# Branch B's tiles: from a turn on TensorE and one store each to a turn in 32x32 blocks on VectorE and four stores each

## The chip, the core and the metric

The kernel runs on one core of a Trainium2 chip. Such a core has engines that run side by side, each through its own list of instructions in order: TensorE (PE in the profile; its weight loads are PEld) multiplies 128x128 blocks into accumulators in PSUM; VectorE (DVE), ScalarE (ACT) and GpSimd (POOL) work on tiles of 128 partitions; SyncE (SP) issues the transfers (DMAs) between the chip's large memory and the tiles. They wait for each other through semaphores. The metric is the device time of one execution in microseconds, the median of several runs.

## What is computed

One layer of an encoder over 2,048 prompt positions and 8 streams of 16 new positions, 2,176 rows of 1,024 channels, or 17 tiles of 128 rows. One projection makes the inputs of three branches; each branch is gated, the three are joined to 1,024 channels, and one output projection with a residual and a normalisation follows. Cut to what matters here:

```python
h = jnp.einsum('btd,de->bte', x, w_in)
a, g_a, u, v, g_b, c1, c2, g_c = jnp.split(h, SPLITS, axis=-1)
y_a = pool_mixer(pool_ext, a, pos0, pool_w, pool_scale)            # 256 channels
v_n = layer_norm(v, gmlp_ln_g, gmlp_ln_b)
y_b = u * spatial_mix(v_n, gmlp_w, gmlp_b)                         # 384 channels
c = c1 * jax.nn.sigmoid(c2)
y_c = conformer_tail(conv_ext, conv_w, conv_b, ...)                # 384 channels, 31 taps
mixed = jnp.concatenate([jax.nn.silu(g_a) * y_a, jax.nn.silu(g_b) * y_b,
                         jax.nn.silu(g_c) * y_c], axis=-1)
out = jnp.einsum('bte,ed->btd', mixed, w_out) + b_out
x_new = layer_norm(ALPHA * x + out, ln_g, ln_b)
```

All inputs are 32-bit floats. Every large product is made of three passes: each operand is split into a high part (a rounded copy, `hi`) and a low part (the rest, `lo`), and hi x hi, lo x hi and hi x lo are summed in one accumulator (`mm3`, lines 208 to 210).

## The kernel before

**Staging.** The 17 tiles are worked in three blocks of 6, 6 and 5 (`BLOCKS`). For each block the program runs through eight groups of projection columns (`GROUPS`): the convolution's inputs (two groups, accumulators `ps_c`), branch A's two (`ps_ga`, `ps_a`), then branch B's v (`ps_v`), its gate (`ps_gb`) and u (`ps_u`), and at last branch C's gate (`ps_gc`). The weights of a group come in pieces through four staging buffers (`stage`), are split by ACT (`whi`, line 152) and VectorE (`wlo`), and are kept in memory (`keep`) for the next blocks. The input columns of the next block come in as `stage<-in_xT` and are split into `xhi` and `xlo` during `ps_gc`.

**Order.** The order of every engine's list is fixed when the program is built. `mm3` advances a clock of TensorE's time; `after(us, fn)` puts a piece of work so many microseconds later on that clock. The convolution's taps (`acc<-cext,cw,acc`, about 1 us each) are kept aside as filling: one is put on VectorE's list whenever a second clock, which sums modelled VectorE times (`Vector`, lines 113 to 130), is behind TensorE's. A `tensor_tensor` of 384 columns counts 0.49 us on it. So any new operation on VectorE moves later taps backwards in the list.

**Branch B.** For tile i of a block, `b_u` multiplies u by the gated mixture (`yb`, rows in the partitions, 384 channels in the columns). For the output projection the channels must be in the partitions. `turn` does this with three 128x128 transposes on TensorE (`tp_b`, line 748); ACT copies the result to `yt` (line 750), and one store puts it into columns 256 to 639 of the tile's row of `mixd` in memory (`store`, line 374). `yb` and `yt` have two buffers each.

**The output stage.** Its start is built into the last block's `ps_gc`: `Mixed` (line 947) loads a tile of `mixd` in two parts of 768 and 256 columns into two staging buffers (line 952) and splits them into `mhi` and `mlo`; then twelve pieces of the output weights come through the same four buffers (`stage<-in_w_out`, line 972; `woxhi`, `woxlo`, `whi`, `wlo`). A load waits until the buffer's last piece is split, so ACT, VectorE and SP go hand in hand here. In ACT's list four of branch C's gates (`sgc`, line 533) stand between these splits. They free accumulators; there are six (`psm`), and the first output product, for two tiles at once, uses four (`ps_o`). SP's list has all loads and stores of the program in one order, among them the last block's convolution states (`o_conv_p`, `o_conv_s`, which wait for ACT's `ncs`).

Of the kernel before, what the change touches and what calls it, by code (L numbers as in the profile page):

```python
# [9 lines left out]
F32 = mybir.dt.float32  # L10
# [4 lines left out]
D = 1024  # L15
P = 128
# [22 lines left out]
BLOCKS = [list(range(0, 6)), list(range(6, 12)), list(range(12, 17))]  # L39
TMAX = 768  # L40
# [33 lines left out]
def encoder_kernel(ctx: ExitStack, tc: tile.TileContext, a):  # L74
    nc = tc.nc
# [5 lines left out]
    pst = ctx.enter_context(tc.tile_pool(name="pst", bufs=2, space=PS))  # L81
# [14 lines left out]
    def after(us, fn):  # L96
        Clock.seq += 1
        heapq.heappush(events, (Clock.pe + us, Clock.seq, fn))
# [35 lines left out]
    vec = Vector()  # L134
# [15 lines left out]
    def split(hi, lo, src, then=None):  # L150

        nc.scalar.copy(hi, src)  # L152

        def low():
            vec.tensor_tensor(out=lo, in0=src, in1=hi.bitcast(F32), op=ALU.subtract)
            if then is not None:
                then()
        if ring.get("ready"):
            after(1.0, low)
        else:  # L160
            low()

    def stage():
        return core.tile([P, TMAX], F32, tag="stage", bufs=STAGE, name="stage")

    class Piece:


        def __init__(self, key, src, cols, keep=None):
            self.key, self.n, self.cols, self.keep = key, src.shape[1], cols, keep  # L170
            self.st = stage()[:, :self.n * cols].rearrange("p (k c) -> p k c", k=self.n)
            nc.sync.dma_start(out=self.st, in_=src)

        def split(self, then=None):
            hi = core.tile([P, 2, 384], F32R, tag="whi", bufs=RING, name="whi")
            lo = core.tile([P, 2, 384], F32R, tag="wlo", bufs=RING, name="wlo")
            split(hi[:, :self.n, :self.cols], lo[:, :self.n, :self.cols], self.st, then)
            ring.setdefault(self.key, []).append((hi, lo))
            if self.keep is not None:
                after(3, lambda: put(self.keep, hi, lo, self.cols))  # L180
# [17 lines left out]
    def wslice(key, k, c0, n):  # L198
        hi, lo = ring[key][k // 2]
        return hi[:, k % 2, c0:c0 + n], lo[:, k % 2, c0:c0 + n]  # L200

    def mm3(outs, kdim=KT, hook=None):

        for k in range(kdim):
            for ps, lhs, rhs in outs:
                lh, ll = lhs(k)
                rh, rl = rhs(k)
                nc.tensor.matmul(ps, lh, rh, start=(k == 0), stop=False)  # L208
                nc.tensor.matmul(ps, lh, rl, start=False, stop=False)  # L209
                nc.tensor.matmul(ps, ll, rh, start=False, stop=(k == kdim - 1))  # L210
            if hook is not None:
                hook(k)
            poll(sum(3 * (o[0].shape[-1] / 2400 + 0.0025) for o in outs))
        Clock.dve = max(Clock.dve, Clock.pe)

    gofs = []
    o = 0
# [28 lines left out]
    class XRow:  # L246
# [14 lines left out]
        def split(self, then=None, halves=False):  # L261
            kp, h = divmod(self.k, 2)
            if h == 0:
                xhi[kp] = core.tile([P, 2, TMAX], F32R, tag=f"xhi{kp}", name=f"xhi{kp}")
                xlo[kp] = core.tile([P, 2, TMAX], F32R, tag=f"xlo{kp}", name=f"xlo{kp}")
            for t in (slice(0, 384), slice(384, self.T)) if halves else (slice(0, self.T),):
                split(xhi[kp][:, h, t], xlo[kp][:, h, t], self.st[:, t], then)

    def xslice(k, t0, n):
        return xhi[k // 2][:, k % 2, t0:t0 + n], xlo[k // 2][:, k % 2, t0:t0 + n]  # L270
# [37 lines left out]
    def C(name, j=0, n=1):  # L308
        return cst[:, CST[name][0] + j:CST[name][0] + j + n]

    ident = const.tile([P, P], F32, name="ident")
# [10 lines left out]
    tmp = tmp_cm.__enter__()  # L322
# [7 lines left out]
    def load_v():  # L330
        nc.sync.dma_start(out=vg, in_=a["gmlp_ln_g"].partition_broadcast(P))
        nc.sync.dma_start(out=vb, in_=a["gmlp_ln_b"].partition_broadcast(P))
        w = raw("wst0", 4)
        nc.sync.dma_start(out=w, in_=a["gw"])
        after(10, lambda: keep_lower(w))
        after(14, lambda: split(*wst, w))
# [32 lines left out]
    mixd = [dram.tile([P, D], F32, name=f"mix{i}") for i in range(NTILE)]  # L369
    stored = {}  # L370

    def store(q, j, src):

        nc.sync.dma_start(out=mixd[q][:, j * P:j * P + src.shape[1]], in_=src)
        stored[q] = stored.get(q, 0) + src.shape[1]

    halo_a = const.tile([P, 2, POOLC], F32, name="halo_a")
    halo_c = const.tile([P, 3, CONVC], F32, name="halo_c")
    nc.gpsimd.memset(halo_a, 0.0)
# [155 lines left out]
    def tail_steps(b):  # L535

        st = {}
# [78 lines left out]
        def pointwise(t0, n, j):  # L616
            nt = n // P
            if j == 0:
                st["m", t0] = cp.tile([P, 3, 3, P], F32, tag="mixs", bufs=1, name="mixs")
            m = st["m", t0]  # L620
            sg = conv_state[(b, "sg")]
            ps = psm.tile([P, 512], F32, tag="mm", name="ps_pw")
            mm3([(ps[:, :n], lambda k: (pwhi[:, k, j * P:(j + 1) * P], pwlo[:, k, j * P:(j + 1) * P]),
                  lambda k: (st["s", t0, k][0][:, :n], st["s", t0, k][1][:, :n]))], 3)
            vec.scalar_tensor_tensor(
                out=m[:, :nt, j, :], scalar=C("pwb", j), op0=ALU.add, op1=ALU.mult,
                in0=ps[:, :n].rearrange("p (i t) -> p i t", t=P),
                in1=sg[:, j, t0:t0 + n].rearrange("p (i t) -> p i t", t=P))
            if j == 2:
                for i in range(nt):  # L630
                    after(2, lambda i=i: store(BLOCKS[b][t0 // P + i], 5, m[:, i].rearrange("p j t -> p (j t)")))

        todo = splits(len(BLOCKS[b]) * P)
        d = cp.tile([P, 3, TMAX], F32, tag="dc", name="dc")
# [10 lines left out]
        for t0, n in todo:  # L645
            for j in range(3):
                yield lambda: gate(t0, n, j)
            for j in range(3):
                yield lambda: pointwise(t0, n, j)
# [84 lines left out]
    def b_u(b, wkey, hook=None):  # L734
        zb = b_state[b]
        for i, q in enumerate(BLOCKS[b]):
            ps = psm.tile([P, 512], F32, tag="mm", name="ps_u")
            mm3([(ps[:, :384], lambda k: xslice(k, i * P, P), lambda k: wslice(wkey, k, 0, 384))],
                hook=hook if i == len(BLOCKS[b]) - 1 else None)

            def out(ps=ps, i=i, q=q):
                yb = tmp.tile([P, 384], F32, tag="yb", bufs=2, name="yb")
                vec.tensor_tensor(out=yb, in0=ps[:, :384], in1=zb[:, i, :], op=ALU.mult)

                def turn():
                    tp = pst.tile([P, 384], F32, tag="tr", name="tp_b")
                    for j in range(3):
                        nc.tensor.transpose(tp[:, j * P:(j + 1) * P], yb[:, j * P:(j + 1) * P], ident)
                    st = tmp.tile([P, 384], F32, tag="yt", bufs=2, name="yt")
                    after(0.4, lambda: nc.scalar.copy(st, tp))  # L750
                    after(2.4, lambda: store(q, 2, st))
                after(3, turn)
            if i < 3:
                after(4, out)
            else:
                out()
# [188 lines left out]
    class Mixed:  # L945

        def __init__(self, q):
            assert stored[q] == D
            self.q = q
            self.st = [(c0, n, stage()[:, :n]) for c0, n in ((0, TMAX), (TMAX, D - TMAX))]  # L950
            for c0, n, st in self.st:
                nc.sync.dma_start(out=st, in_=mixd[q][:, c0:c0 + n])

        def split(self, then=None):
            mhi = op.tile([P, KT, P], F32R, tag="mhi", bufs=3, name="mhi")
            mlo = op.tile([P, KT, P], F32R, tag="mlo", bufs=3, name="mlo")
            for c0, n, st in self.st:
                split(mhi.rearrange("p k t -> p (k t)")[:, c0:c0 + n],
                      mlo.rearrange("p k t -> p (k t)")[:, c0:c0 + n], st, then if c0 > 0 else None)
            ahead[self.q] = (mhi, mlo)  # L960

    wv = a["w_out"].rearrange("(k p) c -> p k c", p=P)
# [199 lines left out]
```

## Time and profile before

| | |
|---|---|
| median of 3 runs | 784.9 us (784.69 to 785.13) |
| the profiled execution | 785.07 us |
| its span, first to last instruction | 783.4 us |
| mean granted TensorE clock | 0.998 |
| DMA | 132.91 MB, mean 170 GB/s |
| `mix<-yt` | 17 stores of 192 KB |

Times in the profile are microseconds from the first instruction; the 1.7 us between span and execution lie around it. A row of a timeline has start, duration, engine, line and operation, output<-inputs, shape, how many (x3), and in brackets how long the engine was idle before and for whom it waited. A row of a group ends in busy time, mean nanoseconds of one, and idle time before. A row of waits is total, count, longest. "SPq" is the issue of a transfer by SP, not the transfer. A row of the page's list of transfers ends in the median time from issue to landing; a tile or line view gives minimum, median and maximum in nanoseconds. Matmul durations overlap their neighbours: what one costs is read from the distance between starts.

### The profile page before, as it was taken

The numbers are of one execution on the slowest core, as the hardware profiler recorded it, in microseconds if no ns is written. First come the engines' busy times: TensorE is split into PE (matmuls) and PEld (weight loads), VectorE is DVE, ScalarE is ACT, GpSimd is POOL, SyncE is SP. The second block draws the span as 40 slices with busy tenths as digits, with TensorE's granted clock in tenths as the row PEclk, the third lists the DMA queues.
The fourth block names the chain that finished last, engine by engine and source line by source line (L and its number), as shares of the span: only waits on it lengthen the run. The fifth ranks groups of instructions, "written<-read, shape, count | busy, mean of one in ns | idle before, by whom it ended". The sixth has DMA issues, their size and how long they took to land.

```text
span 783.4 us, 11336 instructions
## 1 busy us (share of the span) xinstructions
PE 771.0 (98%) x4340; PEld 732.5 (94%) x4340; DVE 611.6 (78%) x899; ACT 203.2 (26%) x379; POOL 144.2 (18%) x172
## 2 busy tenths in 40 slices
PE   8999999999999999999999999999999999999996
PEld 6999999999999999999999999999988878888885
DVE  5799999996489989896047888899764997676665
ACT  5322324222312130220142122031351243131210
POOL 1010112210001011230002200151006254232341
PEclk9999999999999999999999999999999999999999
DMA  7966856459531465413656147362377334435311
GB/s 248 342 216 190 284 208 236 159 188 338 183 109 44 90 231 193 161 45 138 228 169 208 47 94 219 144 209 97 134 239 267 108 134 162 161 110 182 128 69 73
DMA packets 74774, 132.91 MB, mean 170 GB/s; under 512 B 15584, under 2 KB 41312, under 8 KB 74720
## 3 DMA queue, kind: packets, MB, share of 16 engines
q1 hardware_dynamic: 74720, 132.19, 50.6%
q8 instruction: 34, 0.56, 0.3%
q14 instruction: 20, 0.16, 0.1%
HBM read 90.52 MB, written 41.64 MB: 169 GB/s over the span
## 4 chain that ended last, share of the span: by engine, by line
PE 87%; DVE 6%; DMA 3%; SPq 1%; issue 1%; ACT 1%; POOL 1%; POOLq 0%; DVEq 0%; ACTq 0%
PE ps_o L209 7%; PE ps_o L208 7%; PE ps_o L210 7%; PE ps_c L208 4%; PE ps_c L209 4%; PE ps_c L210 4%; PE ps_gb L208 3%; PE ps_gc L208 3%; PE ps_gb L209 3%; PE ps_gc L209 3%; PE ps_gc L210 3%; PE ps_gb L210 3%; PE ps_v L208 3%; PE ps_v L209 3%; PE ps_v L210 3%; PE ps_u L210 3%
## 5 line engine op out<-in xcount | busy, mean ns | idle before, releaser
L131 DVE SCALAR_TENSOR_TENSOR acc<-cext,cw,acc 128x768 f32<-128x768 f32 (+1 forms) x270 | 258.2, 956 | 4.2
L209 PE MATMUL ps_o<-woxlo,mhi 128*128 128x512 f32 (+1 forms) x208 | 80.9, 389 | 0.0
L208 PE MATMUL ps_o<-woxhi,mhi 128*128 128x512 f32 (+1 forms) x208 | 80.8, 389 | 0.0
L208 PE MATMUL ps_c<-xhi,whi 128*128 128x384 f32 (+1 forms) x240 | 79.8, 333 | 0.7 <-ACT xhi L152 0.7
L210 PE MATMUL ps_o<-woxhi,mlo 128*128 128x512 f32 (+1 forms) x208 | 80.4, 387 | 0.0
L209 PE MATMUL ps_c<-xlo,whi 128*128 128x384 f32 (+1 forms) x240 | 78.9, 329 | 0.7 <-DVE xlo L131 0.5
L210 PE MATMUL ps_c<-xhi,wlo 128*128 128x384 f32 (+1 forms) x240 | 78.4, 327 | 0.0
L131 DVE TENSOR_TENSOR xlo<-stage,xhi 128x768 fp32r<-128x768 f32 (+2 forms) x26 | 21.5, 853 | 36.5 <-ACT xhi L152 36.5
L208 PEld LDWEIGHTS ps_o<-woxhi,mhi 128*128 128x128 f32 x208 | 39.1, 188 | 8.3 <-ACT sgc L533 0.2
L209 PEld LDWEIGHTS ps_c<-xlo,whi 128*128 128x128 f32 x240 | 45.2, 188 | 1.7 <-DVE xlo L131 1.7
L208 PEld LDWEIGHTS ps_c<-xhi,whi 128*128 128x128 f32 x240 | 45.3, 189 | 1.6 <-ACT xhi L152 1.3
L210 PEld LDWEIGHTS ps_o<-woxhi,mlo 128*128 128x128 f32 x208 | 39.1, 188 | 8.1
L208 PE MATMUL ps_u<-whi,xhi 128*128 128x384 f32 x136 | 46.6, 342 | 0.0
L209 PEld LDWEIGHTS ps_o<-woxlo,mhi 128*128 128x128 f32 x208 | 39.1, 188 | 7.6
L424 ACT ACTIVATE xr<-xr,onm,ors 128x1024 f32<-128x1024 f32 x16 | 19.9, 1245 | 101.1 <-POOL onm L420 101.1
L210 PE MATMUL ps_u<-whi,xlo 128*128 128x384 f32 x136 | 45.5, 335 | 0.0
L209 PE MATMUL ps_v<-wlo,xhi 128*128 128x384 f32 x136 | 45.5, 334 | 0.0
L208 PE MATMUL ps_v<-whi,xhi 128*128 128x384 f32 x136 | 45.5, 334 | 0.0
L210 PE MATMUL ps_v<-whi,xlo 128*128 128x384 f32 x136 | 45.5, 334 | 0.0
L209 PE MATMUL ps_u<-wlo,xhi 128*128 128x384 f32 x136 | 45.4, 334 | 0.0
L210 PEld LDWEIGHTS ps_c<-xhi,wlo 128*128 128x128 f32 x240 | 45.2, 188 | 0.0
L131 DVE TENSOR_TENSOR xr<-xr,ln_g 128x1024 f32<-128x1024 f32 x16 | 28.5, 1783 | 20.0 <-ACT xr L424 20.0
(212 smaller groups left out, 1944.2 us busy)
## 6 DMA issues: line engine op xcount, KB each, us to landing
whi<-keep SPq DMA_DIRECT2D x34, 384.0 KB, 5.8
wlo<-keep SPq DMA_DIRECT2D x34, 384.0 KB, 6.4
stage<-in_w_in SPq DMA_DIRECT2D x27, 384.0 KB, 5.0
keep<-whi SPq DMA_DIRECT2D x24, 384.0 KB, 3.9
keep<-wlo SPq DMA_DIRECT2D x24, 384.0 KB, 4.1
xr<-in_x_prompt SPq DMA_DIRECT2D x16, 512.0 KB, 5.0
o_y<-xr SPq DMA_DIRECT2D x16, 512.0 KB, 2.9
stage<-keep SPq DMA_DIRECT2D x20, 384.0 KB, 7.6
```

What stands on the lines that cost most here:

```text
L131: return fn(*args, **kw)
L208: nc.tensor.matmul(ps, lh, rh, start=(k == 0), stop=False)
L209: nc.tensor.matmul(ps, lh, rl, start=False, stop=False)
L210: nc.tensor.matmul(ps, ll, rh, start=False, stop=(k == kdim - 1))
L424: nc.scalar.activation(out=out, in_=src, func=AF.Identity, scale=rs, bias=nm_)
```

## The change

VectorE turns `yb` straight into `yt`, in squares of 32x32: each square is transposed where it stands. With s the group of 32 rows and c one of the 12 groups of 32 channels, partition 32 s + i, columns 32 c to 32 c + 31 then hold channel 32 c + i for the rows of s. Four stores, one for each s, take the 32 partitions of s and put their columns, in four pieces of 96, into the four quarters of `mixd`'s partitions. A run in memory is thus 96 numbers (384 bytes) instead of 384 (1,536 bytes). Branch B's columns come last in `mixd` (640 to 1023) and branch C's go to 256 to 639; the reading side undoes the order of the columns while it splits, and the host orders the rows of `w_out` to suit. The two parts of a load are now 640 and 384 columns.

```diff
+    BLK = P // 4
+    BCOL = 5 * P
+
+    def store_turned(q, src):
+        dst = mixd[q].rearrange("(b i) d -> i b d", b=4)
+        for s in range(4):
+            o = BCOL + s * 3 * BLK
+            nc.sync.dma_start(out=dst[:, :, o:o + 3 * BLK],
+                              in_=src[s * BLK:(s + 1) * BLK, :].rearrange("i (b x) -> i b x", b=4))
         stored[q] = stored.get(q, 0) + src.shape[1]
...
-                    after(2, lambda i=i: store(BLOCKS[b][t0 // P + i], 5, m[:, i].rearrange("p j t -> p (j t)")))
+                    after(2, lambda i=i: store(BLOCKS[b][t0 // P + i], 2, m[:, i].rearrange("p j t -> p (j t)")))
...
-                def turn():
-                    tp = pst.tile([P, 384], F32, tag="tr", name="tp_b")
-                    for j in range(3):
-                        nc.tensor.transpose(tp[:, j * P:(j + 1) * P], yb[:, j * P:(j + 1) * P], ident)
-                    st = tmp.tile([P, 384], F32, tag="yt", bufs=2, name="yt")
-                    after(0.4, lambda: nc.scalar.copy(st, tp))
-                    after(2.4, lambda: store(q, 2, st))
-                after(3, turn)
+                st = tmp.tile([P, 384], F32, tag="yt", bufs=2, name="yt")
+                vec.transpose(out=st, in_=yb)
+                after(2, lambda: store_turned(q, st))
...
-            self.st = [(c0, n, stage()[:, :n]) for c0, n in ((0, TMAX), (TMAX, D - TMAX))]
+            self.st = [(c0, n, stage()[:, :n]) for c0, n in ((0, BCOL), (BCOL, D - BCOL))]
...
-                split(mhi.rearrange("p k t -> p (k t)")[:, c0:c0 + n],
-                      mlo.rearrange("p k t -> p (k t)")[:, c0:c0 + n], st, then if c0 > 0 else None)
+                hi, lo = (m[:, c0 // P:(c0 + n) // P] for m in (mhi, mlo))
+                if c0 == BCOL:
+                    hi, lo = (m.rearrange("p c (s t) -> p c s t", s=4) for m in (hi, lo))
+                    st = st.rearrange("p (s c t) -> p c s t", s=4, c=3)
+                else:
+                    st = st.rearrange("p (k t) -> p k t", t=P)
+                split(hi, lo, st, then if c0 > 0 else None)
...
+    wout = x["w_out"][0]
+    wout = np.concatenate([wout[:256], wout[640:],
+                           wout[256:640].reshape(4, 3, 32, D).transpose(1, 0, 2, 3).reshape(384, D)])
```

What the change moves shows at two places. The first is VectorE's list in the first block, from branch B's first tile to the last weights of `ps_gc` (`wlo`). Before:

```order
L131 TENSOR_TENSOR yb<-ps_u,zb 128x384
L131 SCALAR_TENSOR_TENSOR acc_659<-cext_519,cw,acc_659 128x768 x2
L131 TENSOR_TENSOR wlo<-stage,whi 128x768
L131 TENSOR_TENSOR yb<-ps_u,zb 128x384
L131 SCALAR_TENSOR_TENSOR acc_659<-cext_519,cw,acc_659 128x768 x4
L131 TENSOR_TENSOR yb<-ps_u,zb 128x384 x2
L131 SCALAR_TENSOR_TENSOR acc_659<-cext_519,cw,acc_659 128x768 x3
L131 TENSOR_TENSOR yb<-ps_u,zb 128x384
L131 SCALAR_TENSOR_TENSOR acc_659<-cext_519,cw,acc_659 128x768
L131 TENSOR_TENSOR wlo<-stage,whi 128x768 x2
```

The same stretch of VectorE's list after the change, from the first tile's `wlo` on:

```order
L131 TENSOR_TENSOR wlo<-stage,whi 128x768
L131 SCALAR_TENSOR_TENSOR acc_659<-cext_519,cw,acc_659 128x768
L131 TENSOR_TENSOR yb<-ps_u,zb 128x384
L131 STREAM_TRANSPOSE yt<-yb 128x384
L131 SCALAR_TENSOR_TENSOR acc_659<-cext_519,cw,acc_659 128x768 x3
L131 TENSOR_TENSOR yb<-ps_u,zb 128x384
L131 STREAM_TRANSPOSE yt<-yb 128x384
L131 TENSOR_TENSOR yb<-ps_u,zb 128x384
L131 STREAM_TRANSPOSE yt<-yb 128x384
L131 SCALAR_TENSOR_TENSOR acc_659<-cext_519,cw,acc_659 128x768 x2
L131 TENSOR_TENSOR yb<-ps_u,zb 128x384
L131 STREAM_TRANSPOSE yt<-yb 128x384
```

Ahead of these rows the new list has `yb`, a turn and one tap; behind them come the two `wlo`. From the first `yb` to those two there are five turns more, and seven taps where ten were; the three others follow later.

The second place is SP's list at the end of the last block: the stores of its five tiles (mix_205 to mix_209) and the output stage's first loads. Before:

```order
L374 DMA mix_205<-yt 128x384
L511 DMA o_conv_p<-ncs 128x30
L512 DMA o_conv_s<-ncs 128x240
L374 DMA mix_206<-yt 128x384
L374 DMA mix_208<-yt 128x384
L374 DMA mix_207<-yt 128x384
L374 DMA mix_209<-yt 128x384
L952 DMA stage<-mix_193 128x768
L952 DMA stage<-mix_193 128x256
```

SP's list at that place after the change:

```order
L387 DMA mix_205<-yt 32x4x96 x4
L387 DMA mix_206<-yt 32x4x96 x4
L525 DMA o_conv_p<-ncs 128x30
L526 DMA o_conv_s<-ncs 128x240
L387 DMA mix_208<-yt 32x4x96 x4
L387 DMA mix_207<-yt 32x4x96 x4
L387 DMA mix_209<-yt 32x4x96 x4
L961 DMA stage<-mix_193 128x640
L961 DMA stage<-mix_193 128x384
```

Two tiles' stores now stand ahead of the convolution state's instead of one, and twelve instead of four single stores stand between that and the first load of the output stage. On TensorE the only difference is that the 17 groups of three `tp_b` are gone.

More of the change, by code (lines that the diff above doesn't have):

```diff
@@ L375, in store @@
         stored[q] = stored.get(q, 0) + src.shape[1]
+    BLK = P // 4
[6 more added lines that the diff above has]
+                              in_=src[s * BLK:(s + 1) * BLK, :].rearrange("i (b x) -> i b x", b=4))
+        stored[q] = stored.get(q, 0) + src.shape[1]
     halo_a = const.tile([P, 2, POOLC], F32, name="halo_a")
@@ L1134 @@
         "x_prompt": x["x_prompt"][0], "x_sample": xs,
-        "w_in": np.concatenate(parts, axis=1), "w_out": x["w_out"][0],
+        "w_in": np.concatenate(parts, axis=1), "w_out": wout,
         "cst": cst, "gw": x["gmlp_w"][0].transpose(2, 0, 1), "pool_w": x["pool_w"][0],
```

## The prediction

> **What bounds the kernel now.** I began with the page: is one engine busy from end to end?
>
> ```profile
> span 783.4 us, 11336 instructions
> ...
> PE 771.0 (98%) x4340; PEld 732.5 (94%) x4340; DVE 611.6 (78%) x899; ACT 203.2 (26%) x379; POOL 144.2 (18%) x172
> ...
> PE 87%; DVE 6%; DMA 3%; SPq 1%; issue 1%; ACT 1%; POOL 1%; POOLq 0%; DVEq 0%; ACTq 0%
> ```
>
> TensorE is busy for 98% of the span, and the chain that ended last is 87% TensorE. Next came TensorE's own waits, to see whether anything holds it.
>
> ```profile
> PE tp_b L748 <- ACT yt L750: 0.8, 1, 0.8
> PE ps_rstd L600 <- ACT crs L594: 1.2, 1, 1.2
> ...
> PEld ps_o L208 <- ACT sgc L533: 0.2, 1, 0.2
> ```
>
> After the start only two gaps are left, the first of them inside the work that the change removes. So the time is the length of TensorE's stream: what leaves it shortens the kernel one to one, unless something that TensorE now outruns makes it wait. The third row names the likeliest such place: the first output tiles already wait 0.2 us for the branch C gate.
>
> **What is removed.** The tile view gives the pieces, the timeline what they cost in the stream (the 0.27 us is a pipelined length, not a price).
>
> ```profile
> L748 PE MATMUL tp_b<-ident,yb x51: 270/272/299, 159.2 to 555.2; 128*128 128x128 f32 x51
> ...
> 167.53 0.34 PE L210 MATMUL ps_u<-whi,xlo 128*128 128x384 f32 x1
> 167.70 0.49 PE L748 MATMUL tp_b<-ident,yb 128*128 128x128 f32 x3
> ...
> 168.38 0.34 PE L210 MATMUL ps_u<-whi,xlo 128*128 128x384 f32 x1
> ...
> 553.52 0.34 PE L210 MATMUL ps_u<-whi,xlo 128*128 128x384 f32 x1
> ...
> 554.97 0.52 PE L748 MATMUL tp_b<-ident,yb 128*128 128x128 f32 x3 [0.78 <-ACT yt L750]
> ...
> 555.67 0.33 PE L210 MATMUL ps_gc<-xhi,wlo 128*128 128x384 f32 x1
> ```
>
> Matmuls start 0.173 us apart. From L210 at 167.53 to L210 at 168.38 is 0.85 us where three steps take 0.52: one turn costs 0.33 to 0.34. Fifteen such turns are 5.1 us. The last two, 553.52 to 555.67, take 2.15 where 0.52 is due: 1.63 us, of which about 0.95 is the wait for a free yt. **Removed: 6.7 us.** The 17 ACT copies leave an engine that is 26% busy and are worth nothing by themselves.
>
> **What VectorE gets.** Seventeen turns of 128x384. Before shows no such operation. Nearest row: the 128x384 product just ahead of it, 0.55 us; lower end 0.40 (384 columns at the rate of that row without its fixed part), upper end 0.98, the slowest row of this width. I take 0.55.
>
> ```profile
> L131 DVE TENSOR_TENSOR yb<-ps_u,zb x17: 547/551/559, 158.0 to 554.3; 128x384 f32<-128x384 f32 x17
> ...
> L131 DVE TENSOR_TENSOR csum<-acc,acc 128x384 f32<-128x384 f32 x5 | 4.9, 984 | 0.0
> ...
> 170.35 1.01 DVE L131 SCALAR_TENSOR_TENSOR acc<-cext,cw,acc 128x768 f32<-128x768 f32 x1
> 171.28 1.82 DVE L131 TENSOR_TENSOR wlo<-stage,whi 128x768 fp32r<-128x768 f32 x2
> ...
> 173.39 0.33 PE L208 MATMUL ps_gc<-xhi,whi 128*128 128x384 f32 x1
> ```
>
> The tight place is the first block, where VectorE has no idle time and the weights' low halves (wlo) stand behind the turns. Up to those wlo the new order has five turns more (2.75 us) and three convolution taps fewer (3.1 us), so they come no later, at about 172.2 and 173.1. TensorE needs the first of them 12 matmuls into ps_gc, now at 173.39 + 2.08 - 1.7 (five turns gone) = 173.8. It is covered by 1.6 us; at 0.98 a turn it is 0.5 late.
>
> The Trainium skill ("VectorE: DVE Perf Modes", "The three transpose paths") gives 311 ns for one 128x128 turn in 32x32 blocks, in bf16; three of them are an estimate of 0.93 us here, near my upper end. By that price the sum below stays, and this cover is about 0.3 us short; no run here shows it yet.
>
> **What the SP queue gets.** 17 stores become 68. SP issues in order, so each is time for whatever stands behind it.
>
> ```profile
> L374 SPq DMA_DIRECT2D mix<-yt x17: 319/320/767, 161.9 to 556.8; - x17
> ...
> L374 SPq DMA_DIRECT2D mix<-ya x34: 319/424/527, 95.7 to 498.9; - x34
> ...
> L356 SPq DMA_DIRECT2D wss_c<-in_gw x8: 560/580/912, 151.0 to 158.5; - x8
> ...
> L816 SPq DMA_DIRECT2D o_pool_s<-aexts x2: 575/596/617, 461.5 to 481.2; - x2
> ...
> DMA to landing us min/median/max: 7.0/7.3/7.6
> ...
> L388 SPq DMA_DIRECT2D cexts<-in_state_conv x3: 618/2011/2277, 254.3 to 257.1; - x3
> ```
>
> A store of whole rows takes 0.32 to 0.42 us. The new ones are 32x4x96, with a step inside each partition, like wss_c, o_pool_s and cexts: 0.58 typically. With 0.04 between instructions I take 0.62 from store to store; ends 0.46 (the rows of ya) and 0.95 (the slowest wss_c).
>
> ```profile
> 172.63 3.55 SPq L254 DMA_DIRECT2D stage<-in_xT  x4
> ...
> 186.40 1.57 ACT L152 CAST xhi<-stage 128x768 fp32r<-128x768 f32 x2 [3.67 <-PE ps_gc L210]
> ...
> stage<-keep SPq DMA_DIRECT2D x20, 384.0 KB, 7.6
> stage<-in_xT SPq DMA_DIRECT2D x14, 384.0 KB, 4.3
> ...
> 350.56 2.11 SPq L195 DMA_DIRECT2D stage<-keep  x4
> 363.05 13.69 SPq L374 DMA_DIRECT2D mix<-yt  x5
> ...
> 376.19 0.33 PE L208 MATMUL ps_gc<-xhi,stage 128*128 128x384 f32 x1
> ```
>
> In the first two blocks this is hidden. In the first, three or four more microseconds of stores stand ahead of the next block's xT loads; they go out near 175.3 instead of 172.6 and land 4.3 later, while their casts wait for TensorE until 186.4 (now 2.0 earlier). In the second, two of the four loads of gate weights (stage<-keep) now stand behind the first tile's stores: SP waits for its turn until about 359.2, issues four, and sends the loads near 361.7 instead of 351.5. They land 7.6 later, at 369.3, and are first read six matmuls (1.0 us) into ps_gc, at 376.2 + 1.0 - 3.7 = 373.5. Cover 4 us.
>
> In the **last block** the queue decides. There SP waits for an ACT copy (ncs), then issues three tiles' stores, then the loads for the output stage.
>
> ```profile
> 552.30 4.81 SPq L374 DMA_DIRECT2D mix<-yt  x4
> 557.20 8.27 SPq L952 DMA_DIRECT2D stage<-mix  x6
> ...
> stage<-mix SPq DMA_DIRECT2D x3, 384.0 KB, 3.7
> mix<-yt SPq DMA_DIRECT2D x1, 192.0 KB, 2.0
> ...
> 562.55 0.38 ACT L533 ACTIVATE sgc<-ps_gc 128x256 f32<-128x256 f32 x1 [2.38 <-PE ps_gc L210]
> 562.83 2.17 ACT L152 CAST mhi<-stage 128x768 fp32r<-128x768 f32 x4
> ...
> 577.26 1.41 ACT L533 ACTIVATE sgc<-ps_gc 128x384 f32<-128x384 f32 x4
> ```
>
> By then 14 turns are gone, so the stores start at 552.30 - 4.75 = 547.55. Twelve at 0.62 end at 555.0. (The last turn needs the yt of the first of these tiles: its fourth store goes out at 549.4, lands 2.0 later, and with the turn that is 551.95, before SP is free at 552.5. So SP sets it.) To keep step with TensorE, stage<-mix would have to go out at 557.20 - 6.7 = 550.5; it is 4.5 late. Some is covered: it landed 3.7 after issue, at 560.9, and ACT took it only at 562.83, behind a gate. That is 1.9. The remaining 2.6 us runs on through ACT's chain (each cast there waits for a load that waits for a buffer) to the four gates at 577.26. The third run of the output product needs the accumulator that they free, and that wait is the 0.2 of above: no slack. **Given back: 2.6 us.**
>
> The output stage's reads are re-cut from 768+256 to 640+384 columns; as many columns in as many instructions, the second part read in steps of 32 columns.
>
> ```profile
> L131 DVE TENSOR_TENSOR mlo<-stage,mhi 128x768 fp32r<-128x768 f32 x17 | 21.6, 1272 | 4.3 <-ACT mhi L152 4.3
> ...
> L131 DVE TENSOR_TENSOR mlo<-stage,mhi 128x256 fp32r<-128x256 f32 x17 | 7.1, 417 | 0.0
> ```
>
> VectorE spends 1.7 us a tile there, and TensorE about 11 (48 matmuls of 512 columns, 0.23 apart). I take zero; if the steps cost a tenth, 0.17 us a tile stays under the 11, and only the ps_rstd wait of 1.2 us, which hangs on VectorE, could grow by some tenths.
>
> **The sum.** 785.07 (profiled execution: span 783.4 and 1.7 around it) - 6.7 + 2.6 = 781.0. The median of the runs is 784.9, 0.17 lower: **780.8 us**.
>
> **The rivals.**
> 1. *All covered.* SP or ACT catches up and TensorE never waits: 784.9 - 6.7 = 778.2. For it: TensorE waits nowhere else. Against: the sgc wait is there already.
> 2. *Cheap stores.* At 0.46 the last turn's wait decides: 547.55 + 1.4 + 2.0 + 0.55 = 551.5, four more stores to 553.4, 2.9 late, 1.0 given back: 779.2.
> 3. *VectorE becomes the bound* at about 1 us a turn: 0.5 us lost in the first block, perhaps as much again in the last, on top of the forecast: 781.8 to 783.
> 4. *Slower: SP's issue.* If a store with an inner step takes 0.96 us or more, the twelve end at 559.1, 8.6 late, and the 6.7 is gone. At 1.2 us they end at 562.0: 11.5 late, 9.6 given back, 787.8. For it: the cexts row, 2.0 and 2.3 us. Against: those loads have 1,024 runs each, the new stores 128. Between 0.83 and 1.1 the difference is too small to measure. The Trainium skill ("DMA: Bandwidth & Descriptors", "Specifications") asks for 512 B or more per transfer for full rate, and these runs have 384. The row of o_pool_s agrees in kind: 60 KB in 60-byte runs land after 7.0 to 7.6 us, where 192 KB in 1,536-byte runs take 2.0. Priced by that row (5.3 us more for 1,024 runs, so 0.7 for 128) a store lands at 2.7, the last turn ends at 552.65, and the sum moves by 0.1.
>
> **How the numbers follow.** Chances: forecast (store 0.55 to 0.8) 0.45; rival 1 0.15; rival 2 0.20; rival 3 0.08; no measurable gain 0.06; slower 0.06. A measurement of this kernel tells about 0.2% (1.6 us) from no change. Faster by more: 0.45 + 0.15 + 0.20 + 0.08 = 0.88. The range runs from rival 1, less 0.2, to the forecast with stores of 0.8 us (twelve end at 557.2: 4.8 given back, 783.0): 778.0 to 783.2.
>
> **What would show it.** No tp_b in the profile, and TensorE's stream 5.8 us shorter; STREAM_TRANSPOSE near 0.55 us; the new stores near 0.58 in SP's rows; TensorE waiting 2 to 3 us for sgc at the start of the output stage, and nowhere else new. A wait on wlo in the first block would speak for rival 3; no wait on sgc for rival 1; several waits on whi, xlo or stage for rival 4. The forecast is wrong if stores cost ACT's chain nothing, or if TensorE's two remaining gaps grow by more than a microsecond.

## The result, and the profile after

The changed kernel's median is 779.93 us (778.51 to 781.09, 4 runs) beside 784.99 us for the kernel before (784.69 to 785.13, 4 runs): a ratio of 0.9935, 95% interval 0.9923 to 0.9948. Two later sets of runs gave 0.9919 (0.9905 to 0.9933) and 0.9937 (0.9924 to 0.9951). The medians of the three sets lie 5 to 7 us below those of the kernel before; the forecast was 780.8.

The page of the changed kernel (the execution of 778.51 us, the shortest of the four): the span, the busy times, and the engines' shares of the chain that ended last.

```profile
span 776.8 us, 11275 instructions
...
PE 765.0 (98%) x4289; PEld 727.4 (94%) x4289; DVE 621.1 (80%) x916; ACT 194.9 (25%) x362; POOL 144.0 (19%) x172
...
PE 92%; DMA 2%; DVE 2%; POOL 1%; SPq 1%; ACT 1%; issue 0%; POOLq 0%; DVEq 0%; ACTq 0%
```

TensorE has 51 instructions fewer, VectorE 17 more, ScalarE 17 fewer; TensorE is still the bound. Its waits after the start, in the same execution:

```profile
PE ps_rstd L614 <- ACT crs L608: 1.1, 1, 1.1
PE ps_o L208 <- ACT sgc L547: 0.8, 1, 0.8
...
PEld ps_o L208 <- ACT sgc L547: 1.3, 1, 1.3
```

The wait inside the turns is gone, that for `crs` is as it was, and the one for branch C's gate at the start of the output stage, 0.2 us before, has grown to 0.8 us of TensorE's time.

Where the time went is read from the start of the same matmul in both traces. Two more of TensorE's rows of before (the third, at 555.67, was shown above):

```profile
159.03 0.33 PE L210 MATMUL ps_u<-whi,xlo 128*128 128x384 f32 x1
...
577.91 0.39 PE L208 MATMUL ps_o<-woxhi,mhi 128*128 128x512 f32 x1
```

The same three in the changed kernel:

```profile
158.07 0.33 PE L210 MATMUL ps_u<-whi,xlo 128*128 128x384 f32 x1
...
548.04 0.33 PE L210 MATMUL ps_gc<-xhi,wlo 128*128 128x384 f32 x1
...
571.26 0.50 PE L208 MATMUL ps_o<-woxhi,mhi 128*128 128x512 f32 x1 [0.83 <-ACT sgc L547]
```

Ahead of the first turn the changed kernel is already 0.96 early: that is the start-up, and no work of the change. Behind the last turn it is 7.63 early, so the turns were worth 6.67 us. At the gate 1.0 is given back (6.65 early), and from there to the end nothing changes.

The turned tiles, their stores and what waits for them, by tile, in the changed kernel (durations in ns):

```profile
L387 SPq DMA_DIRECT2D mix<-yt x68: 302/430/1940, 159.8 to 552.3; - x68
L131 DVE STREAM_TRANSPOSE yt<-yb x17: 578/578/581, 157.7 to 549.9; 128x384 f32<-128x384 f32 x17
...
  DMA mix<-yt: 2.5, 3
...
DMA to landing us min/median/max: 1.6/1.7/7.9
```

A turn takes 0.578 us, the issue of a store has a median of 0.43, and a store of 128 runs lands after a median of 1.7. Three turns waited, 2.5 us in all, for a free `yt`. SP's timeline in the last block, and ScalarE's chain behind it, both of the changed kernel:

```profile
546.71 7.17 SPq L387 DMA_DIRECT2D mix<-yt  x12
553.92 5.45 SPq L961 DMA_DIRECT2D stage<-mix  x6
```

```profile
554.92 0.39 ACT L547 ACTIVATE sgc<-ps_gc 128x256 f32<-128x256 f32 x1 [2.38 <-PE ps_gc L210]
556.96 1.18 ACT L152 CAST mhi<-stage 128x640 fp32r<-128x640 f32 x2 [1.65 <-DMA stage<-mix]
...
561.41 1.14 ACT L152 CAST mhi<-stage 128x640 fp32r<-128x640 f32 x2 [1.28 <-DMA stage<-mix]
563.88 0.83 ACT L152 CAST woxhi<-stage 128x768 fp32r<-128x768 f32 x1 [1.32 <-DMA stage<-in_w_out]
...
570.73 1.42 ACT L547 ACTIVATE sgc<-ps_gc 128x384 f32<-128x384 f32 x4
```

Twelve stores, then the loads, then ScalarE idle for 1.65 us in front of the first `mhi`. Two rows of ScalarE's chain in the kernel before (the others were shown above):

```profile
567.85 1.14 ACT L152 CAST mhi<-stage 128x768 fp32r<-128x768 f32 x2 [2.84 <-DMA stage<-mix]
570.52 1.78 ACT L152 CAST woxhi<-stage 128x768 fp32r<-128x768 f32 x2 [1.54 <-DMA stage<-in_w_out]
```

To see how late each step is, 7.63 is taken from its time before. The loads go out 4.35 us late (553.92 against 557.20 - 7.63), the first `mhi` starts 1.76 late (556.96 against 562.83 - 7.63), the third tile's 1.19 (before at 567.85), the first `woxhi` 0.99 (before at 570.52), the gates 1.10 (before at 577.26).

### The profile page after: what moved, and what is told of

Read it like the earlier page. It is cut to its first block, busy times and chain, and to the rows that moved or that the text cites. A ratio compares the mean times of both kernels' runs of the same rounds, so it can differ in the third digit from the quotient of the medians.

```text
span 776.8 us, 11275 instructions
## 1 busy us (share of the span) xinstructions
PE 765.0 (98%) x4289; PEld 727.4 (94%) x4289; DVE 621.1 (80%) x916; ACT 194.9 (25%) x362; POOL 144.0 (19%) x172
## 4 chain that ended last, share of the span: by engine, by line
PE 92%; DMA 2%; DVE 2%; POOL 1%; SPq 1%; ACT 1%; issue 0%; POOLq 0%; DVEq 0%; ACTq 0%
PE ps_o L208 7%; PE ps_o L209 7%; PE ps_o L210 7%; PE ps_c L208 6%; PE ps_c L209 6%; PE ps_c L210 6%; PE ps_gb L208 3%; PE ps_gb L209 3%; PE ps_gb L210 3%; PE ps_v L209 3%; PE ps_v L208 3%; PE ps_v L210 3%; PE ps_u L210 3%; PE ps_u L209 3%; PE ps_u L208 3%; PE ps_gc L210 2%
## 5 line engine op out<-in xcount | busy, mean ns | idle before, releaser
L152 ACT CAST whi<-stage 128x768 fp32r<-128x768 f32 (+1 forms) x39 | 29.9, 770 | 65.4 <-PE ps_u L210 30.7
```

## Experiments

In the trace of each run the start of every matmul was compared with that of the same one in before's trace. "Start" is how far the kernel was behind before (+) or ahead (-) at 159.03; the other columns are what it lost (+) or gained (-) in the stretch, in us, with the marks in before's times: the three blocks (to about 555.8), the gate (to 577.91), the rest of the convolution (to 636.95, `ps_rstd`), the output tiles (to 775.56).

| kernel | ratio to before | start | blocks | gate | to 637 | to the end |
|---|---|---|---|---|---|---|
| changed, first trace | 0.9935 | -0.97 | -6.67 | +0.99 | +0.04 | 0.00 |
| changed, second | 0.9919 | +0.35 | -6.67 | +1.42 | +0.22 | 0.00 |
| changed, third | 0.9937 | +0.57 | -6.67 | +1.27 | -0.40 | -0.01 |
| whole rows | 0.9921 | -0.62 | -6.67 | +0.02 | +0.16 | -0.01 |
| late stores | 0.9926 | -0.62 | -6.67 | +1.07 | +0.17 | +1.79 |
| ScalarE's stores | 0.9975 | -0.41 | -6.67 | +2.98 | +2.61 | 0.00 |
| six yt | 0.9923 | +0.08 | -6.67 | +2.36 | -0.13 | 0.00 |
| ScalarE's stores, six yt | 0.9915 | -0.18 | -6.67 | +0.20 | -0.09 | 0.00 |
| the same again | 0.9913 | +0.15 | -6.67 | 0.00 | -0.31 | 0.00 |
| double turn | 0.9964 | -0.63 | -5.14 | +2.11 | -0.48 | 0.00 |
| eight stores | 1.0151 | -0.50 | +5.46 | +7.45 | +1.12 | -0.01 |
| eight stores, six yt | 1.0157 | 0.00 | +3.39 | +7.06 | +1.07 | 0.00 |

Single executions of one kernel lay up to 6 us apart (the kernel before: 784.36 to 787.29 in 11 runs beside the second trace), and the intervals are 0.0012 to 0.0022 of the ratio, 1 to 1.7 us, to either side. The times alone cannot tell a wait of one microsecond; the columns can, each for the one execution that was traced.

**The changed kernel twice more** (labels e1_again and e9_changed_third), no edit.

> The changed kernel once more, for a second trace and more times. Theory (SP's stores): TensorE's stream is 6.7 us shorter, and what is missing to 778.2 (784.9 less 6.7) is the wait for branch C's gate at the start of the output stage, 0.9 us in the first trace and more in slower executions: median 779.3 to 780.5, executions 2 us apart, and in this trace (execution time less 777.6) is lost at that one place. Rival (start-up): the executions differ in the first 60 us, where the first trace was 0.86 us ahead of the kernel before, and the gate's wait is the same 0.9 in every trace.

> The changed kernel a third time, beside the two below. Theory: the stream of matmuls is 6.7 us shorter, the gate at the start of the output stage waits 0.8 to 1.4 us, and the rest of the difference between executions lies in the first 60 us or in stretches without any wait: ratio to the kernel before 0.992 to 0.9935.

Medians 778.61 (778.06 to 780.44) and 780.03 (779.33 to 781.48). The gate's wait on TensorE was 1.3 and 1.1 us after 0.8, the turns were worth 6.67 each time to the hundredth, and the start differed by 1.5 us between three executions of one program. Both theories of the first expectation held in part: the loss behind the start is at the gate, and the spread is mostly the start-up. The first median fell below the 779.3 to 780.5 that was expected, and the second ratio, 0.9937, lies just above 0.992 to 0.9935.

**Whole rows** (e2_whole_rows): one store, in place of four. It writes the turned squares where they stand; the kernel leaves out the placing of branch B's channels.

```diff
-        for s in range(4):
-            o = BCOL + s * 3 * BLK
-            nc.sync.dma_start(out=dst[:, :, o:o + 3 * BLK],
-                              in_=src[s * BLK:(s + 1) * BLK, :].rearrange("i (b x) -> i b x", b=4))
+        nc.sync.dma_start(out=mixd[q][:, BCOL:], in_=src)
```

> The turned tile is stored by one transfer of whole rows instead of four (the squares stay where they stand, so branch B's part of the output is left unplaced). VectorE's turns, the order of the channels and the re-cut loads stay. Theory (SP's stores): in the last block three stores stand ahead of the output stage's loads instead of twelve, 9 x 0.47 = 4.2 us less than the 3.4 they are late, so no new gate wait: 778.2, less the 0.2 that the kernel before waited there; executions within 0.5 us of one another. Rival (VectorE's turns or the re-cut loads cost the missing 1.7 us): as the changed kernel, 779.9.

Median 779.15 (778.23 to 780.24), where 778.2 and executions within 0.5 us were expected: on the time alone it is not told from the changed kernel. In the trace the gate's loss is 0.02, and no row of TensorE's waits names the gate. SP, then ScalarE, in this kernel:

```profile
547.01 3.17 SPq L384 DMA_DIRECT2D mix<-yt  x3
550.23 7.71 SPq L957 DMA_DIRECT2D stage<-mix  x6
```

```profile
555.54 2.18 ACT L152 CAST mhi<-stage 128x640 fp32r<-128x640 f32 x4
...
570.10 1.41 ACT L543 ACTIVATE sgc<-ps_gc 128x384 f32<-128x384 f32 x4
```

The loads go out 3.7 us earlier than in the changed kernel (4.0 beside its own TensorE, whose start was 0.35 later), and the first `mhi` follows the gate ahead of it without a pause. So the gate's wait comes from the four-fold stores; the turns on VectorE and the re-cut loads cost nothing at that place.

**Late stores** (e4_late_stores): the last block's third and fifth tile are stored behind the output stage's first four loads. The buffers of the blocks' tiles, which the output stage takes over, are given up only behind these stores.

```diff
+    late = []
...
-                after(2, lambda: store_turned(q, st))
+                if q in BLOCKS[-1][2:3] + BLOCKS[-1][4:]:
+                    late.append(lambda: store_turned(q, st))
+                else:
+                    after(2, lambda: store_turned(q, st))
...
     loads = Loader(jobs)
+    for fn in late:
+        fn()
...
```

> Two of the last block's five tiles are stored after the output stage's first four loads instead of before them; all else as in the changed kernel. Theory (SP's stores): the first loads go out 3.8 us earlier, about 549.5 to 550.2, which is in step with TensorE (550.5); the gate's wait falls to at most the 0.2 of the kernel before: 777.6 to 778.4, and the executions draw together. Rival (the gate waits for something else in ScalarE's chain): no change, 779.9.

Median 779.45 (777.98 to 781.17), and the gate still lost 1.07: the expectation fell, though its first half came true. SP's and VectorE's timelines of this kernel, and VectorE's of the one with whole rows, whose blocks ran at the same times to 0.01 us:

```profile
547.05 1.79 SPq L388 DMA_DIRECT2D mix<-yt  x4
549.20 1.76 SPq L961 DMA_DIRECT2D stage<-mix  x4
551.01 4.64 SPq L388 DMA_DIRECT2D mix<-yt  x8
```

```profile
557.25 2.49 DVE L131 TENSOR_TENSOR mlo<-stage,mhi 128x640 fp32r<-128x640 f32 x4
```

```profile
556.30 2.50 DVE L131 TENSOR_TENSOR mlo<-stage,mhi 128x640 fp32r<-128x640 f32 x4
```

The loads went out at 549.20, in step. But the last of the late stores landed at 557.04, and `mlo` began 0.95 us later than with whole rows, right behind that. The output stage's tiles lie in the memory that the blocks' tiles leave, `yt` among them, so a wait for buffers took the place of a wait for loads. That the landing is what held `mlo` is argued from these times, and it is not all of the 1.07: a later load of output weights in this trace landed 4.1 us after its issue, where it took 3.5 with whole rows. The next runs take both waits away.

**ScalarE's stores** (e5_scalar_stores), **the same with six yt buffers** (e8_scalar_yt6, e10_scalar_yt6_again), and **six yt buffers alone** (e11_yt6_alone). The first part of the diff moves the last block's stores to ScalarE, the second lets `yt` go round three pairs of buffers in place of one.

```diff
-            nc.sync.dma_start(out=dst[:, :, o:o + 3 * BLK],
+            eng = nc.scalar if q in BLOCKS[-1] else nc.sync
+            eng.dma_start(out=dst[:, :, o:o + 3 * BLK],
...
-                st = tmp.tile([P, 384], F32, tag="yt", bufs=2, name="yt")
+                st = tmp.tile([P, 384], F32, tag=("yt", "vhi", "vlo")[i % 3], bufs=2, name="yt")
```

> The last block's twenty stores of turned tiles are issued by ScalarE, which idles there for 5 us before each gate, instead of by SP; the other twelve tiles as in the changed kernel. The run with the late stores still lost 0.9 us: the theory now says that there the loads were early enough, and the output stage's low halves (mlo), which lie in the memory of yt, waited for the late stores to land at 557.0. Here nothing stands ahead of the loads and the stores land early: loads out at 548 to 550, mlo no later than in the run with whole rows (about 556.3 in a trace of the same start), the gate's wait gone: TensorE in the output stage 6.5 to 6.7 us ahead of where it would be with the turns on TensorE, total 6.7 below the kernel before, ratio 0.9915. Rival (the gate hangs on something that neither run changed, such as the traffic of the stores): the wait stays 0.9 to 1.3, ratio 0.993.

> ScalarE issues the last block's stores, and yt has six buffers: both waits that the change brought are taken away at once. Theory: VectorE's 2.4 us of waits for a free yt go, but nothing late hung on them, so the time is that of the run with ScalarE's stores alone, ratio 0.991 to 0.992. Rival (the yt waits did cost): 1 to 2 us faster than that run.

> ScalarE's stores and six yt buffers once more, beside the changed kernel itself. Theory: no gate wait again, so 0.9 to 1.3 us ahead of the changed kernel in the same set of runs; since single executions differ by 2 us, the two medians may be anything from 0 to 2.5 us apart, and the trace decides: TensorE's lead over the changed kernel has to appear at the output stage's third run of products and nowhere else. Rival: no difference there.

> The changed kernel with six yt buffers instead of two; all stores stay with SP. Theory (SP's queue makes the gate late): VectorE's waits for a free yt go (2.4 us), the loads of the output stage still stand behind twelve stores, the gate waits 0.5 to 1.3. Rival (the last turn's wait for a free yt holds the last four stores and with them the loads): the loads go out 1 us or more earlier relative to TensorE and the gate's wait is 0 to 0.3.

ScalarE's stores alone: 782.82 (782.16 to 784.2), slower than the changed kernel by 3 to 4 us, against the expectation. ScalarE's queue, VectorE, TensorE's wait and its granted clock (windows: us, busy time, clock, DMA share, GB/s) in that kernel:

```profile
546.78 9.00 ACTq L388 DMA_DIRECT2D mix<-yt  x11
```

```profile
553.41 0.58 DVE L131 STREAM_TRANSPOSE yt<-yb 128x384 f32<-128x384 f32 x1 [3.98 <-DMA mix<-yt]
...
560.36 2.49 DVE L131 TENSOR_TENSOR mlo<-stage,mhi 128x640 fp32r<-128x640 f32 x4
```

```profile
PE ps_o L208 <- ACT sgc L548: 2.8, 1, 2.8
```

```profile
567.00:574.00 7.00, 4.18 (x25) 0.93 0.77 257
574.00:580.00 6.00, 6.00 (x15) 0.51 0.71 207
```

Eleven stores that take 0.44 us each needed 9.0. The loads of SP now run beside them, and the stores landed after up to 3.8 us instead of 1.7. The program tells landings by eight semaphores, which all its transfers use in turn, and a store goes out only when the transfer that had its semaphore before has landed: one store went out at 549.47 behind a landing at 549.44, one at 551.76 behind a landing at 551.74. So the last turn waited 4.0 us for its `yt`, every tap behind it came later, and `mlo` began at 560.36. TensorE waited 2.8 us, and then ran at half clock for some microseconds, which cost another 2.6.

With six buffers no turn waits for a store. The expectation that nothing late hung on these waits fell: the median is 4.6 us below that of two buffers. The two runs of that kernel are the fastest of the study, 778.24 (777.71 to 779.39) and 778.27 (777.03 to 780.04), and its gate lost 0.20 and 0.00. Whether it beats the changed kernel is not settled by the times (0.9913, interval 0.9898 to 0.9929, beside 0.9937, 0.9924 to 0.9951, in one set); the traces show 0.8 to 1.4 us less lost at the gate than the three of the changed kernel.

Six buffers with SP's stores: 779.39 (778.52 to 780.77). VectorE's waits for `yt` are gone, and the gate still waits, 2.2 us on TensorE, more than the 0.5 to 1.3 that were expected. SP, TensorE's wait, and ScalarE's last cast ahead of the gates:

```profile
547.75 7.14 SPq L387 DMA_DIRECT2D mix<-yt  x12
554.94 5.66 SPq L961 DMA_DIRECT2D stage<-mix  x6
```

```profile
PE ps_o L208 <- ACT sgc L547: 2.2, 1, 2.2
...
572.62 0.62 ACT L152 CAST whi<-stage 128x512 fp32r<-128x512 f32 x1 [0.82 <-DMA stage<-in_w_out]
```

So the wait for `yt` is not the cause in the changed kernel; SP's twelve stores, 7.1 us without any wait of VectorE, are. The size of the loss is another matter. Set against TensorE's stream, the loads were as late here (4.3 us) as in the three traces of the changed kernel (4.2 to 4.35), and the first `woxhi` was 1.5 late beside their 1.0 to 1.6. But the load for the cast above landed 4.3 us after its issue, where theirs took 3.1 to 3.2, and the gates behind it came 2.5 late. One slow landing is thus worth as much here as the whole loss of the changed kernel; why it was slow stays open.

**Eight stores** (e3_eight_stores), and **with six yt buffers** (e6_eight_stores_yt6).

```diff
+        H = BLK // 2
         for s in range(4):
             o = BCOL + s * 3 * BLK
-            nc.sync.dma_start(out=dst[:, :, o:o + 3 * BLK],
-                              in_=src[s * BLK:(s + 1) * BLK, :].rearrange("i (b x) -> i b x", b=4))
+            for i in (0, H):
+                nc.sync.dma_start(out=dst[i:i + H, :, o:o + 3 * BLK],
+                                  in_=src[s * BLK + i:s * BLK + i + H, :].rearrange("i (b x) -> i b x", b=4))
```

> Eight stores of 16 partitions for each tile instead of four of 32, the same bytes to the same places. Theory (cost per store on SP): twelve more stores ahead of the output stage's loads, at 0.35 to 0.47 us each 4.2 to 5.6 us, none of it covered any more: 779.9 + 4.2 to 5.6 = 784.1 to 785.5, the gain nearly gone, with 5 to 6 us of waits for gates and splits at the start of the output stage. Rival (the cost lies in the 128 short runs of a tile, which stay as many): 779.9, within 0.5.

> Eight stores for each tile again, but six yt buffers instead of two. With two, VectorE waited 17.3 us for stores before it could turn, and TensorE lost 4.8 us on wlo in the first block, 6.4 on gates at the start of the second, some 8 at the output stage. Theory (two mechanisms): VectorE's wait for a free yt cost the 4.8; SP's queue (the next block's input columns go out at 183 instead of 174) the rest. Then the 4.8 goes and the 6.4 and the 8 stay: 793. Rival A (all of it is VectorE's wait): 784 to 786, what was first expected of eight stores. Rival B (all of it is SP's queue): 798 as with two buffers, with the wait on wlo unchanged.

Medians 798.03 (793.84 to 799.85) and 797.21 (795.72 to 799.22): 12 to 13 us slower than before, where 784 to 785.5 was expected. TensorE's waits in the first, its granted clock there behind the wait for `wlo` (window, length, busy time, clock, DMA share, GB/s), and ScalarE at the start of the second block in the second:

```profile
PE ps_c L208 <- ACT sgc L549: 3.3, 1, 3.3
PE ps_o L208 <- ACT sgc L549: 2.9, 1, 2.9
PE ps_gc L210 <- DVE wlo L131: 2.9, 1, 2.9
PE ps_o L208 <- ACT woxhi L152: 2.2, 1, 2.2
```

```profile
176.00:178.00 2.00, 1.33 (x6) 0.85 0.25 51
178.00:180.00 2.00, 2.00 (x8) 0.50 0.26 53
180.00:182.00 2.00, 2.00 (x11) 0.79 0.18 33
182.00:184.00 2.00, 2.00 (x13) 1.00 0.54 184
```

```profile
203.91 0.83 ACT L152 CAST xhi<-stage 128x768 fp32r<-128x768 f32 x1 [11.48 <-DMA stage<-in_xT]
204.64 1.63 ACT L549 ACTIVATE sgc<-ps_gc 128x384 f32<-128x384 f32 x4
```

The gates that TensorE waits for at the start of the second block stand in ScalarE's list behind a cast that waited 11.5 us for the next block's input columns, which SP could not send before it had issued the stores. Six buffers removed the wait for `wlo`, 2.9 us and the half clock behind it, and 2.1 of the blocks' loss; the wait at the start of the second block grew from 3.3 to 6.0, and the time did not change. SP's queue is what holds this kernel up, and the wait for `yt` is only one of the places where it showed. The expectation of 793 for the second run missed that a wait taken away ahead of a later one of the same cause comes back there.

**Double turn** (e7_double_turn).

```diff
                 vec.transpose(out=st, in_=yb)
+                nc.vector.transpose(out=st, in_=yb)
```

> Every turn is made twice on VectorE, 17 x 0.58 = 9.9 us more there; taps and all else stay in their places. Theory (VectorE has cover but in the first block): the second pair of wlo, ready 1.3 to 1.5 us before it is needed, stands behind five more turns, 2.9 us, of which 0.8 replaces a wait for yt: TensorE waits 0.6 to 0.9 us for wlo in the first block and about the same at the gate of the output stage as before; 0.6 to 1.5 us above the changed kernel run beside it. Rival (VectorE has slack everywhere): no wait on wlo, no difference. Rival (VectorE is the bound): near 9.9 us more.

Median 781.49 (780.89 to 783.79), 1.5 to 3 us above the changed kernel, not ten. Its waits on TensorE:

```profile
PE ps_o L208 <- ACT sgc L547: 2.0, 1, 2.0
...
PE ps_gc L210 <- DVE wlo L131: 1.2, 1, 1.2
```

Of 9.9 us of additional work on VectorE 1.5 reach TensorE in the first block, where a wait of 0.6 to 0.9 was expected and one of 1.2 came. The gate lost 2.1, where about as much as in the changed kernel was expected. The loads go out 0.6 us later beside TensorE, but the gate also lost 2.4 with six buffers and single turns, so this trace does not show that the second turns cost anything there. The cover in the first block is there, and it is short.

## Why the prediction was right, and where its numbers were off

**The removed turns.** Forecast 6.7 us, measured 6.67 in every trace in which the stores did not hold up the blocks. Reading the cost of a turn from the distance between the matmuls around it, and not from its 0.27 us, was right.

**VectorE's turn.** Forecast 0.55, measured 0.578. The Trainium skill's price ("VectorE: DVE Perf Modes", "The three transpose paths"), worked out as an estimate of 0.93, was too high for this 32-bit tile; the trace decides. The first block's cover, forecast 1.6 us, shows in the changed kernel's rows of VectorE and TensorE:

```profile
170.93 0.92 DVE L131 TENSOR_TENSOR wlo<-stage,whi 128x768 fp32r<-128x768 f32 x1
...
173.15 0.33 PE L210 MATMUL ps_gc<-xhi,wlo 128*128 128x384 f32 x1
```

The first `wlo` is ready at 171.85, and TensorE, which began `ps_gc` at 170.72, reads it at 173.15, 14 matmuls later and not 12 as the prediction counted: 1.3 us. One of the turns ahead of it had waited 0.85 us for a free `yt`, a wait that the prediction did not have. The second `wlo` is ready 1.5 us ahead of its first reader. The double turn, in which TensorE waits for the first, confirms that this is all there is.

**SP's stores.** Forecast 0.62 us from one to the next, and loads 4.5 us late. A store's issue takes 0.43, 0.475 from start to start, as in the rival of cheap stores. Yet twelve took 7.17, 0.60 each, and the loads went out 4.35 late. Twelve issues are 5.7 us; the rest is one pause of 0.4 for VectorE and one issue of 1.6 us, the last store of all. That came again in the other two traces of this kernel (1.6 both), with six `yt` (1.6) and, one store earlier, with double turns (1.8). In each of these traces a transfer of the DMA queue that the profile calls `instruction` runs at that moment; in the changed kernel's it lasts from 552.05 to 553.49, beside the issue from 552.29 to 553.88. The DMA queues there, from 552 to 553.6 (packets, MB, share of the engines):

```profile
q8 instruction: 1, 0.02, 5.6%
```

With ScalarE's stores and six `yt` a long issue (1.65 and 1.03) on ScalarE's queue meets the same transfer. That the transfer is what held the issue is not shown, since no run moves it. The size was right, its composition was not, and that is luck: the price of a store was too high, and the long issue made up for most of it. Without it the loads would have gone out about 3.2 us late (an estimate, 4.35 less the 1.16 by which this issue is longer than the others).

**What ScalarE's chain covers.** This is the step that was off: "The remaining 2.6 us runs on through ACT's chain". Measured: 1.0 to 1.4 given back. Two things made it less. The loads landed 3.0 us after issue instead of 3.7, so the chain began 1.76 late and not 2.6. And along the chain the lateness shrank to 1.10 at the gates, since the third tile's loads landed after 2.8 us where before's took 3.1, and its first cast and subtraction are 640 columns wide instead of 768. A wait does not run one to one through a chain whose links wait for transfers. It can also grow there: with six `yt` and the loads equally late 2.4 was given back, close to the forecast, through one load that landed late. With 1.0 to 1.4 in place of 2.6 the sum is 785.07 - 6.67 + 1.0 to 1.4, less 0.2 for the median: 779.2 to 779.6; 779.93 was measured, and 778.61 and 780.03 in the later sets.

**No cost from the re-cut reads.** With whole rows, which keep the re-cut, 0.02 is lost at the gate, and 0.16 and -0.01 in the two stretches behind it.

**The rivals.** All covered did not happen to the changed kernel; it is what six buffers with ScalarE's stores give (778.2 and 778.3 against 778.2). Cheap stores had the right price for a store and the right time (779.2) with the wrong reason, since the last turn did not set the loads, and they were 4.35 us late and not 2.9. VectorE as the bound did not happen at 0.578 a turn, and at two turns a tile, 1.16, the first block lost 1.5 us, about what its rule gives (five times 0.61 more, less the cover of 1.6), though the cover was shorter and the wait of 0.85 for `yt` was not in the rule. The slower case was mis-sized: eight stores a tile, 3.8 us of issue where its condition asked for four of 0.96, should have cost the 6.7 and gave a kernel 12 us slower than before. It looked at the last block alone, while the same queue holds the next block's input columns, and 10 to 12 us were lost in the blocks.

## What to carry to other kernels

Work taken off the busiest engine is worth its distance in that engine's stream; what comes back is found by following the queue that got the work instead, up to the first instruction on the busy engine with no slack. On the way the lateness changes at each link that waits for a transfer: 4.3 us at the loads became 1.0 to 2.4 at the gate, so one trace does not give its size. One transfer cut into several costs the issuing queue that many issues, and everything behind them: look at each place where that queue holds loads for the next stage, not only at the last. A buffer count that is harmless with one issuing engine can become the bound when the stores move to another.

## What the runs showed of the hardware

- **A long wait costs more than itself.** Around the end of waits of 2.8 and 2.9 us TensorE's granted clock fell to 0.50 to 0.51 for several microseconds (the windows above): the wait of 2.9 for `wlo` lost about 4.8 in all, that of 2.8 for the gate 5.6. Single waits of 2.0 and 2.2 us (double turn, six `yt`) left the clock at 1.00; one of 2.2 in the eight-store kernel was followed by 0.50, so the length of the wait alone does not decide. The Trainium skill describes such a half-rate state after about 3.4 us without work, and the return after about as long of work ("TensorE: Matmul & The Clock Gate", "What's actually happening"); the traces agree in kind, with a drop after somewhat less (2.2, 2.8 and 2.9 us).
- **Issue is paid per transfer, not per byte.** Stores of 24 KB (eight a tile) had a median issue of 0.42 us, of 48 KB 0.43; stores of 192 KB in the kernel with whole rows had a median of 0.32, and the first of a run of 48 KB stores took 0.30.
- **No cost of short runs was seen.** 48 KB in runs of 384 bytes landed after 1.7 us, 192 KB in runs of 1,536 bytes after 2.0. The Trainium skill ("DMA: Bandwidth & Descriptors", "Specifications") asks for 512 bytes for full rate; at this size it did not show, but no run has the same size in both forms, so a small cost stays open.
- **Eight transfers under way, by this program.** At no issue in the traces were eight earlier ones still under way, whichever engine issued it. The traces show eight semaphores for all landings, used in turn by SP's and ScalarE's transfers together, and no issue ahead of the landing that had its semaphore before. That is how this program is built; whether the chip has such a limit is not shown.
- **A stretch without a wait that ran slower.** In the trace with late stores the matmuls of the output tiles came up to 2% further apart from about 680 to 770 us (times of before), 1.79 us in all over the output tiles, at a granted clock of 1.00; no other trace shows it, and its cause is open.
